# A four-layer diffusion backbone step: the product with the values of an attention unit is issued behind the first scores of the next unit

## The chip, the cores and the metric

The kernel runs on one core of one Trainium2 chip. The metric is the device time of one execution in microseconds (us), the median of three runs. Beside the runs there is one profiled execution, whose trace gives the start, the length and the wait of each instruction.

## What is computed

One inference step of a trunk of four layers with the same weights for 128 context tokens and 512 latent tokens (640 together, width 1024, 16 heads of 64); 128 further context tokens are cached as keys and values. Each layer is: modulated norm, a token mixer, a gated residual, a modulated norm, SwiGLU, a gated residual.

Here `op` is the mixer's output for the context tokens, which see context keys alone, and `os_` that of the latent tokens, which see a selection of latent keys and all cached context keys in one softmax. The mixers of layers 0 to 3 are neighbourhood attention, a sliding window, latent attention with low-rank keys, and grouped-query attention.

```python
for li in range(DEPTH):
    mp = adaln(c_ctx[None, :], w_mod[li], b_mod[li])
    ms = adaln(c, w_mod[li], b_mod[li])
    hp = modulate(rms_norm(xp, norm1_g[li]), mp[0], mp[1])
    hs = modulate(rms_norm(xs, norm1_g[li]), ms[0], ms[1])
    ...
    xp = xp + mp[2] * op
    xs = xs + ms[2] * os_
    xp = xp + mp[5] * swiglu(modulate(rms_norm(xp, norm2_g[li]), mp[3], mp[4]), ffn_w_gate[li], ffn_w_up[li], ffn_w_down[li])
    xs = xs + ms[5] * swiglu(modulate(rms_norm(xs, norm2_g[li]), ms[3], ms[4]), ffn_w_gate[li], ffn_w_up[li], ffn_w_down[li])

def joint_softmax(parts, sink=None):
    s = jnp.concatenate(parts, axis=-1) if len(parts) > 1 else parts[0]
    m = jnp.max(s, axis=-1, keepdims=True)
    ...
    p = jnp.exp(s - m)
    p = p / den
```

## The kernel before

All matrix products are made from pairs of rounded numbers (a high and a low part), so that one product is three matmuls: high by high, low by high, high by low. In the profile they are `whi,hh`, `wlo,hh`, `whi,hl` (or `hh,whi` and so on), and all of them have line 271, the helper `mm`.

The attention of a layer is a loop over 16 **units** (`units`). A unit is a pair of heads and one half of the 512 latent queries: unit u is group u//4, pair u//2 % 2, half u % 2 (`half_pair`). It has four **blocks** (`blocks`, one method for each kind of mixer), each of one head and 128 queries:

1. the scores of the block, queries by keys, into a PSUM tile `S` (`S<-k,q`; in layer 2 `S<-k,qn` and `S<-kpe,qpe`);
2. the softmax on VectorE, ScalarE and GpSimd, which leaves `p`;
3. TensorE turns `p` into `tp` (PSUM, `tp<-consts,p`, line 1009), and ScalarE copies `tp` to `pt` (line 285).

Behind the four blocks comes the **product with the values** (`pv`): `sm<-pt,v` into one PSUM tile `sm`, 16 to 20 matmuls that all read `pt`. For odd units the attention of the context tokens follows in the same tile (`prompt_group`, then `sm<-ptp,v`). Its result, `o`, is copied out by `put_o`. PSUM holds in layers 0 and 1 three `S`, two `tp` and three `sm` tiles, in layers 2 and 3 two `S` of two banks, two `tp` and two `sm`.

Other work is placed between the blocks. `job(gen, n, t0, t1)` spreads the n steps of a generator evenly from time t0 to t1, where the time is the unit plus a quarter per block; `tick` runs before each block. These are the projections of the next group (in layer 2 the `sm<-whi,hh` products of 384 columns), the preparation of keys and queries (`prep_group`, `prep_pair`, transposes `tp<-consts,ktok` and `tp<-consts,qs`), the parts of the output projection (`out_part`, `sm<-hh,whi` of 320 columns, which read the finished `o` of pairs 0 to 4, made ready by `acts`), and parts of the modulation (`mod_parts`, `sm<-rawm,cond`). The keys of a pair are doubled to both halves of the partitions by copies between SBUF tiles on the queue of SyncE (SP), `k<-k`, and the first scores of the next pair read them.

What order the engines get is not the order of the code: a scheduler of the framework emits, on each engine, the instruction with the best priority among those that it holds ready at that time. `high_priority(offset=AHEAD)` pulls an attention block ahead of the filler by 100 places, and `issue_after(x)` forbids an instruction before x. `run_of` binds the matmuls of one accumulation together: the first is placed, and the others follow it.

Of the kernel before, what the change touches and what calls it, by code (L numbers as in the profile page):

```python
# [17 lines left out]
NL = 512  # L18
NP = 128
T = 640  # L20
# [242 lines left out]
class Net:  # L263
# [6 lines left out]
    def mm(self, out, lhsT, rhs, start, stop):  # L270
        return self.nc.tensor.matmul(out, lhsT=lhsT, rhs=rhs, start=start, stop=stop, skip_group_check=True)  # L271
# [593 lines left out]
class Attn:  # L865
# [5 lines left out]
    def __init__(self, net, L):  # L871
        self.net, self.L, self.nc = net, L, net.nc
        self.o, self.V, self.hd = {}, {}, {}
        self.sink = None
        self.jobs, self.events = [], {}
        self.fast = True
# [32 lines left out]
    def units(self):  # L909
        self.fast = False  # L910
        for u in range(16):
            self.half_pair(u // 4, u // 2 % 2, u % 2)
        self.tick(16)
# [180 lines left out]
    def half_pair(self, g, pr, hf):  # L1094
        net = self.net
        u = 4 * g + 2 * pr + hf
        own = self.prompt_group(g, pr) if hf else None
        vals = self.blocks(g, pr, hf, u)
        with net.tc.high_priority(offset=AHEAD):
            o = net.ps()  # L1100
            net.run_of(self.pv(o[:, :256], vals) + (self.pv(o[:, 256:384], own) if hf else []))
            self.put_o(self.o_tile(2 * g + pr), o[:, :256], hf)
            if hf:
                self.put(self.o_tile(2 * g + pr), slice(NL, T), o[:, 256:384])
# [47 lines left out]
class Full(Attn):  # L1152


    def blocks(self, g, pr, hf, u):
# [3 lines left out]
        for b in range(4):  # L1159
            jj, e = b // 2, b % 2  # L1160
            self.tick(u + b / 4)
            with net.tc.high_priority(offset=AHEAD):
                s = net.ps("S")
                for half in range(2):
                    self.scores(4 * g + 2 * pr + e, s[:, half, :320], 2 * hf + jj, half * 320, half * 320 + 320)
                p = self.softmax(s[:, :, :320], T)
# [11 lines left out]
class Mha:  # L1178
# [4 lines left out]
    def body(self):  # L1183
# [11 lines left out]
        self.job(self.acts(self.direct), 5, 12.5 - lead, 13.5 - lead)  # L1195
        self.job(net.out_part(L, 0), 16, max(13.5 - lead, 10) + (0 if L else 0.5), 16)
# [3 lines left out]
        else:  # L1200
            self.at(13.5 - lead, self.load_x)
# [44 lines left out]
class Na(Mha, Attn):  # L1246
# [77 lines left out]
    def blocks(self, g, pr, hf, u):  # L1324
        net = self.net
        pt = self.tile([P, 2, 3, 256], "pt", 2)
        for jj in range(2):
            j = 2 * hf + jj
            w0 = self.win[j][0]
            for e in range(2):  # L1330
# [3 lines left out]
                with net.tc.high_priority(offset=AHEAD):  # L1334
                    s = net.ps("S")[:, :384]
                    self.score(s[:, :256], q, k[:, 0, w0:w0 + 256], k[:, 1, w0:w0 + 256])
                    self.score(s[:, 256:], q, k[:, 0, T:], k[:, 1, T:])
                    p = self.softmax(s, 384, bias[:, (0, 1, 1, 2)[j]])
# [84 lines left out]
class Swa(Gqa, Attn):  # L1423
# [11 lines left out]
    def blocks(self, g, pr, hf, u):  # L1435
        net, k = self.net, self.kg[g]
        pt = self.tile([P, 2, 4, 256], "pt", 2)
        for jj in range(2):
# [10 lines left out]
            for e in range(2):  # L1449
                self.tick(u + (2 * jj + e) / 4)  # L1450
                h = 4 * g + 2 * pr + e
                with net.tc.high_priority(offset=AHEAD):
# [3 lines left out]
                    self.score(s[:, co:co + P], q, k[:, 0, NL:T], k[:, 1, NL:T])  # L1456
                    p = self.softmax(s, w + P, m, (self.sink[0][:, h:h + 1], self.sink[1][:, h:h + 1]))
# [297 lines left out]
```

## Time and profile before

| | us |
|---|---|
| median of 3 runs | 3218.72 |
| lowest and highest | 3214.39, 3223.7 |
| profiled execution | 3216.05 |
| its span (first to last instruction) | 3214.0 |
| attention of layer 0 | 46 to 400 |
| attention of layer 1 | 905 to 1145 |
| attention of layer 2 | 1635 to 1965 |
| attention of layer 3 | 2485 to 2745 |

The mean granted clock of TensorE in the profiled execution is 0.976 of full speed. Between the four stretches of attention lie the output projection, the SwiGLU and the first projections of the next layer. A row of the timeline is a run of like instructions of one engine: its start, the time it took, the instruction and its count, and in brackets how long the engine stood idle before it and which write released it.

### The profile page before, as it was taken

The numbers are of one execution on the slowest core, as the hardware profiler recorded it, in microseconds if no ns is written. First come the engines' busy times: TensorE is split into PE (matmuls) and PEld (weight loads), VectorE is DVE, ScalarE is ACT, GpSimd is POOL, SyncE is SP. The second block draws the span as 40 slices with busy tenths as digits, with TensorE's granted clock in tenths as the row PEclk, the third lists the DMA queues.
The fourth block names the chain that finished last, engine by engine and source line by source line (L and its number), as shares of the span: only waits on it lengthen the run. The fifth ranks groups of instructions, "written<-read, shape, count | busy, mean of one in ns | idle before, by whom it ended". The sixth has DMA issues, their size and how long they took to land.

```text
span 3214.0 us, 57273 instructions
## 1 busy us (share of the span) xinstructions
PE 3029.7 (94%) x21901; PEld 2841.6 (88%) x21901; DVE 2161.6 (67%) x4522; ACT 1528.5 (48%) x3264; POOL 607.1 (19%) x691
## 2 busy tenths in 40 slices
PE   7998989999999989999986899899999999899999
PEld 6997879999988779999985778899998878799999
DVE  5555587666586768585768766867575775875765
ACT  4555454333356755242446664434243576543432
POOL 2553200000044420000025542000001553100000
PEclk9998999999999999999998999999999999899999
DMA  8346563232433342222211224522233111132322
GB/s 265 97 123 208 176 224 102 70 92 94 147 102 128 112 155 76 83 83 76 87 53 37 63 75 143 170 89 80 83 132 118 52 32 32 53 99 70 96 66 86
DMA packets 159027, 331.41 MB, mean 103 GB/s; under 512 B 18592, under 2 KB 40480, under 8 KB 158752
## 3 DMA queue, kind: packets, MB, share of 16 engines
q1 hardware_dynamic: 155584, 323.46, 32.3%
q8 instruction: 173, 2.83, 0.4%
q10 hardware_dynamic: 3168, 4.28, 0.4%
q14 instruction: 102, 0.84, 0.1%
HBM read 303.86 MB, written 4.28 MB: 96 GB/s over the span
## 4 chain that ended last, share of the span: by engine, by line
PE 81%; DVE 8%; DMA 5%; ACT 3%; issue 1%; POOL 1%; SPq 0%; DVEq 0%; ACTq 0%; POOLq 0%
PE big L271 53%; PE sm L271 18%; PE S L271 6%; PE tp L1009 3%; DMA rawm<-in_wmod 3%; DMA k<-k 1%; PE tp L271 1%; DMA raw<-in_wall 1%; DVE st L1030 1%; ACT p L1031 1%; DVE x L603 1%; DVE wlo L319 1%; ACT pt L285 0%; DVE qs L958 0%; DVE hl L999 0%
## 5 line engine op out<-in xcount | busy, mean ns | idle before, releaser
L271 PE MATMUL big<-hh,whi 128*128 128x320 f32 x2720 | 825.4, 313 | 11.7 <-ACT hh L645 5.6
L271 PE MATMUL big<-hl,whi 128*128 128x320 f32 x2720 | 829.0, 311 | 6.3 <-DVE hl L649 3.6
L271 PE MATMUL big<-hh,wlo 128*128 128x320 f32 x2720 | 821.0, 310 | 0.0
L318 ACT CAST whi<-raw 128x512 fp32r<-128x512 f32 (+2 forms) x636 | 383.3, 607 | 709.2 <-PE big L271 554.0
L271 PEld LDWEIGHTS big<-hh,whi 128*128 128x128 f32 x2720 | 508.8, 190 | 25.8 <-ACT hh L645 7.8
L271 PEld LDWEIGHTS big<-hl,whi 128*128 128x128 f32 x2720 | 510.1, 189 | 12.0 <-DVE hl L649 6.2
L271 PEld LDWEIGHTS big<-hh,wlo 128*128 128x128 f32 x2720 | 508.2, 189 | 0.1
L319 POOL TENSOR_TENSOR wlo<-raw,whi 128x512 fp32r<-128x512 f32 (+2 forms) x148 | 196.7, 1342 | 1634.0 <-ACT whi L318 1600.6
L319 DVE TENSOR_TENSOR wlo<-raw,whi 128x512 fp32r<-128x512 f32 (+1 forms) x488 | 325.1, 670 | 142.1 <-ACT whi L318 136.1
L318 ACT CAST whi<-sum 128x512 fp32r<-128x512 f32 x352 | 217.6, 619 | 300.1 <-PE big L271 264.6
L271 PE MATMUL big<-ah,wlo 128*128 128x320 f32 x1408 | 329.1, 309 | 0.0
L271 PE MATMUL big<-ah,whi 128*128 128x320 f32 x1408 | 329.0, 310 | 0.0
L271 PE MATMUL big<-al,whi 128*128 128x320 f32 x1408 | 328.6, 309 | 0.0
L319 DVE TENSOR_TENSOR wlo<-sum,whi 128x512 fp32r<-128x512 f32 x352 | 240.8, 684 | 54.5 <-ACT whi L318 52.9
L1041 POOL TENSOR_SCALAR p<-p,st 128x640 f32<-128x640 f32 (+2 forms) x256 | 197.7, 778 | 285.2 <-DVE st L1040 172.0
L603 DVE SCALAR_TENSOR_TENSOR x<-big,mod,x 128x128 f32<-128x128 f32 (+2 forms) x384 | 146.2, 432 | 150.7 <-PE big L271 150.3
L271 PEld LDWEIGHTS big<-ah,whi 128*128 128x128 f32 x1408 | 237.3, 188 | 1.3 <-issue 0.8
L271 PEld LDWEIGHTS big<-al,whi 128*128 128x128 f32 x1408 | 237.3, 188 | 0.3
L271 PEld LDWEIGHTS big<-ah,wlo 128*128 128x128 f32 x1408 | 237.3, 188 | 0.2
L271 PE MATMUL sm<-whi,hh 128*128 128x256 f32 (+1 forms) x770 | 225.1, 297 | 1.7 <-DVE qs L287 1.1
L271 PE MATMUL sm<-wlo,hh 128*128 128x256 f32 (+1 forms) x770 | 223.3, 292 | 0.2 <-POOL wlo L319 0.2
L271 PE MATMUL sm<-whi,hl 128*128 128x256 f32 (+1 forms) x770 | 223.1, 291 | 0.0
(260 smaller groups left out, 5419.3 us busy)
## 6 DMA issues: line engine op xcount, KB each, us to landing
raw<-in_wall SPq DMA_DIRECT2D x676, 256.0 KB, 2.6
rawm<-in_wmod SPq DMA_DIRECT2D x176, 512.0 KB, 5.8
k<-k SPq DMA_DIRECT2D x38, 384.0 KB, 4.2
bias<-in_nabias SPq DMA_DIRECT2D x16, 576.0 KB, 7.2
raw<-in_wmod SPq DMA_DIRECT2D x32, 256.0 KB, 5.7
qpe<-pes SPq DMA_DIRECT2D x56, 80.0 KB, 2.1
raw<-in_wall SPq DMA_DIRECT2D x32, 128.0 KB, 2.1
out_y<-x ACTq DMA_DIRECT2D x8, 320.0 KB, 2.2
```

The source lines that it names most:

```text
L271: return self.nc.tensor.matmul(out, lhsT=lhsT, rhs=rhs, start=start, stop=stop, skip_group_check=True)
L318: self.nc.scalar.copy(hi, raw)
L319: eng.tensor_tensor(lo, raw, hi.bitcast(F32), ALU.subtract)
L603: self.last = self.nc.vector.scalar_tensor_tensor(xs, halves[b][:, p0:p1], self.mcol(L, i, d, c), xs, ALU.mult, ALU.add)
L1009: self.nc.tensor.transpose(out, in_, self.net.ident)
L1030: nc.vector.tensor_reduce(nm, s, axis=AX.XY, op=ALU.max, negate=True)
L1031: nc.scalar.activation(p.rearrange("p (a b) -> p a b", a=2), s, AF.Exp, bias=nm, accum_out=den)
L1041: nc.gpsimd.tensor_scalar(p, p, rd, 1.0, ALU.mult, ALU.mult)
```

## The change

The product with the values is no longer issued at the end of its unit. `half_pair` wraps it, with the copies that empty it, in a function `product` and keeps that in `late`. In the next unit each `blocks` calls `scores_done` behind the scores of each block; the first such call takes `product` from `late` and runs it, with `issue_after` on the last matmul of those scores. The last unit's product runs behind the loop with no such condition. `self.scored` is reset with each unit.

Since `o` of a pair is thus complete half a block to one unit later, two jobs and the reload of `x` have new times: `acts` runs from 13 - lead to 14 - lead (it was 12.5 to 13.5), and `out_part` and `load_x` start at 14 - lead (13.5 before).

```diff
@@ -268,7 +268,8 @@
 
 
     def mm(self, out, lhsT, rhs, start, stop):
-        return self.nc.tensor.matmul(out, lhsT=lhsT, rhs=rhs, start=start, stop=stop, skip_group_check=True)
+        self.last_mm = self.nc.tensor.matmul(out, lhsT=lhsT, rhs=rhs, start=start, stop=stop, skip_group_check=True)
+        return self.last_mm
 
     def run_of(self, mms):
 
@@ -873,6 +874,7 @@
         self.o, self.V, self.hd = {}, {}, {}
         self.sink = None
         self.jobs, self.events = [], {}
+        self.late, self.scored = [], None
         self.fast = True
 
     def run(self):
@@ -910,6 +912,7 @@
         self.fast = False
         for u in range(16):
             self.half_pair(u // 4, u // 2 % 2, u % 2)
+        self.late.pop()()
         self.tick(16)
 
     def tile(self, shape, tag, bufs=1, dt=F32):
@@ -1096,12 +1099,27 @@
         u = 4 * g + 2 * pr + hf
         own = self.prompt_group(g, pr) if hf else None
         vals = self.blocks(g, pr, hf, u)
-        with net.tc.high_priority(offset=AHEAD):
-            o = net.ps()
-            net.run_of(self.pv(o[:, :256], vals) + (self.pv(o[:, 256:384], own) if hf else []))
-            self.put_o(self.o_tile(2 * g + pr), o[:, :256], hf)
-            if hf:
-                self.put(self.o_tile(2 * g + pr), slice(NL, T), o[:, 256:384])
+
+        def product():
+            with net.tc.high_priority(offset=AHEAD):
+                o = net.ps()
+                mms = self.pv(o[:, :256], vals) + (self.pv(o[:, 256:384], own) if hf else [])
+                if self.scored is None:
+                    net.run_of(mms)
+                else:
+                    with net.tc.issue_after(self.scored.ins):
+                        net.run_of(mms)
+                self.put_o(self.o_tile(2 * g + pr), o[:, :256], hf)
+                if hf:
+                    self.put(self.o_tile(2 * g + pr), slice(NL, T), o[:, 256:384])
+        self.scored = None
+        self.late.append(product)
+
+    def scores_done(self):
+
+        if self.late:
+            self.scored = self.net.last_mm
+            self.late.pop()()
 
     def put_o(self, dst, o, hf):
         self.put(dst, slice(hf * 256, (hf + 1) * 256), o)
@@ -1163,6 +1181,7 @@
                 s = net.ps("S")
                 for half in range(2):
                     self.scores(4 * g + 2 * pr + e, s[:, half, :320], 2 * hf + jj, half * 320, half * 320 + 320)
+                self.scores_done()
                 p = self.softmax(s[:, :, :320], T)
                 for kt in range(5):
                     if n % 4 == 0:
@@ -1192,13 +1211,13 @@
             self.job(self.prep_pair(g, 0), self.pp, 4 * g - mid, 4 * g - end)
         for g in range(4):
             self.job(self.prep_pair(g, 1), self.pp, 4 * g, 4 * g + 1)
-        self.job(self.acts(self.direct), 5, 12.5 - lead, 13.5 - lead)
-        self.job(net.out_part(L, 0), 16, max(13.5 - lead, 10) + (0 if L else 0.5), 16)
+        self.job(self.acts(self.direct), 5, 13 - lead, 14 - lead)
+        self.job(net.out_part(L, 0), 16, 14 - lead + (0 if L else 0.5), 16)
         if L:
             if L == 1:
                 self.job(net.mod_parts(2, 0, 4096, self.ap), 9, 0, 16)
         else:
-            self.at(13.5 - lead, self.load_x)
+            self.at(14 - lead, self.load_x)
             self.job(net.mod_parts(0, 2048, 6144, self.ap), 9, 7, 16)
         self.now(self.prep_group(0), self.prep_pair(0, 0))
         self.units()
@@ -1335,6 +1354,7 @@
                     s = net.ps("S")[:, :384]
                     self.score(s[:, :256], q, k[:, 0, w0:w0 + 256], k[:, 1, w0:w0 + 256])
                     self.score(s[:, 256:], q, k[:, 0, T:], k[:, 1, T:])
+                    self.scores_done()
                     p = self.softmax(s, 384, bias[:, (0, 1, 1, 2)[j]])
                     tp = net.ps("tp")[:, :384]
                     for kt in range(3):
@@ -1454,6 +1474,7 @@
                     q = self.hd[h][:, j * P:(j + 1) * P]
                     self.score(s[:, lo:lo + w], q, k[:, 0, t0 * P:t1 * P], k[:, 1, t0 * P:t1 * P])
                     self.score(s[:, co:co + P], q, k[:, 0, NL:T], k[:, 1, NL:T])
+                    self.scores_done()
                     p = self.softmax(s, w + P, m, (self.sink[0][:, h:h + 1], self.sink[1][:, h:h + 1]))
                     tp = net.ps("tp")[:, :w + P]
                     for i, c in enumerate(cols):
```

The same matmuls are issued, in another order. The rows below are the queue of TensorE as it is written into the program; each row is a line, an operation, the tiles and the shape of the output, with a count where like instructions follow each other (the trace shows a matmul of the kinds `S<-k`, `sm<-pt,v` and `sm<-rawm,cond` as two, so 10 here are x20 there). Of the 60 places between two units of a layer, the next unit's first scores stood ahead of the product in 44 before, and stand ahead of it in all 60 now.

Layer 2, from unit 3 to unit 4 (the units 7 to 8 and 11 to 12 are alike). Before, TensorE's queue from the transposes of `ktok` on:

```order
L1009 MATMUL tp<-consts,ktok 128x128 x6
L1009 MATMUL tp<-consts,p 128x128 x12
L271 MATMUL sm<-pt,v 64x256 x10
L271 MATMUL sm<-ptp,v 64x128 x2
L271 MATMUL sm<-whi,hh 128x384
L271 MATMUL sm<-wlo,hh 128x384
L271 MATMUL sm<-whi,hl 128x384
L271 MATMUL sm<-whi,hh 128x384
L271 MATMUL sm<-wlo,hh 128x384
L271 MATMUL sm<-whi,hl 128x384
L271 MATMUL S<-k,qn 128x320 x2
L271 MATMUL S<-kpe,qpe 128x320
```

And in the changed kernel, from the third of the six products on:

```order
L271 MATMUL sm<-whi,hl 128x384
L271 MATMUL sm<-whi,hh 128x384
L271 MATMUL sm<-wlo,hh 128x384
L271 MATMUL sm<-whi,hl 128x384
L1012 MATMUL tp<-consts,p 128x128 x12
L271 MATMUL S<-k,qn 128x320 x2
L271 MATMUL S<-kpe,qpe 128x320
L271 MATMUL S<-k,qn 128x320 x2
L271 MATMUL S<-kpe,qpe 128x320
L271 MATMUL sm<-pt,v 64x256 x10
L271 MATMUL sm<-ptp,v 64x128 x2
L271 MATMUL S<-k,qn 128x320 x2
```

The six products stand ahead of the transposes `tp<-consts,p` now, and the first four rows of scores of unit 4 (its first block) stand between these and the product with the values `sm<-pt,v`, which came ahead of everything before.

Layer 0, from unit 11 to unit 12, TensorE's queue. Before:

```order
L271 MATMUL sm<-hl,whi 128x320
L271 MATMUL sm<-hh,wlo 128x320
L271 MATMUL sm<-pt,v 64x256 x2
L271 MATMUL sm<-pt,vs 64x128 x4
L271 MATMUL sm<-pt,v 64x128 x4
L271 MATMUL sm<-ptp,v 64x128 x2
L271 MATMUL S<-k,q 128x256 x2
L271 MATMUL S<-k,q 128x128 x2
```

In the changed kernel:

```order
L271 MATMUL sm<-hl,whi 128x320
L271 MATMUL sm<-hh,wlo 128x320
L271 MATMUL S<-k,q 128x256 x2
L271 MATMUL S<-k,q 128x128 x2
L271 MATMUL sm<-pt,v 64x256 x2
L271 MATMUL sm<-pt,vs 64x128 x4
L271 MATMUL sm<-pt,v 64x128 x4
L271 MATMUL sm<-ptp,v 64x128 x2
```

Here the rows `sm<-hh,whi` and its like are the output projection. The first scores of unit 12 moved from behind the product of unit 11 to ahead of it, and of the 24 projections that stood ahead of that product, behind the last transposes of unit 11, 12 are left there.

Layer 1, unit 8, TensorE's queue (`pp` belongs to the context tokens). Before, directly behind the transposes of `qs`:

```order
L1009 MATMUL tp<-consts,p 128x128 x11
L271 MATMUL S<-k,q 128x256 x2
L271 MATMUL S<-k,q 128x128 x2
L1009 MATMUL tp<-consts,pp 128x128 x2
L271 MATMUL S<-k,q 128x256 x2
L271 MATMUL S<-k,q 128x128 x2
L271 MATMUL S<-k,q 128x384 x2
L271 MATMUL S<-k,q 128x128 x2
L1009 MATMUL tp<-consts,p 128x128 x4
L271 MATMUL sm<-pt,v 64x256 x6
L271 MATMUL sm<-pt,v 64x128 x2
L271 MATMUL sm<-rawm,cond 32x256 x16
```

In the changed kernel:

```order
L1012 MATMUL tp<-consts,qs 128x128 x5
L271 MATMUL sm<-rawm,cond 32x256 x16
L1012 MATMUL tp<-consts,p 128x128 x11
L1012 MATMUL tp<-consts,pp 128x128 x2
L271 MATMUL S<-k,q 128x256 x2
L271 MATMUL S<-k,q 128x128 x2
L271 MATMUL S<-k,q 128x256 x2
L271 MATMUL sm<-pt,v 64x256 x6
L271 MATMUL sm<-pt,v 64x128 x2
```

The modulation product `sm<-rawm,cond` moved ahead of the transposes of `p`, directly behind those of `qs`, and two rows of scores stand between the transposes and the product of the unit before.

On SP the copies `k<-k` keep their place relative to the work that makes the keys. At the three places of layer 2 a load of weights (`raw<-in_wall`), which was issued behind them, now stands ahead of them.

## Rows read from the trace of the kernel before

**Rows 1.** Page, part 1: busy us, share of span, instructions.

```profile
PE 3029.7 (94%) x21901; PEld 2841.6 (88%) x21901; DVE 2161.6 (67%) x4522; ACT 1528.5 (48%) x3264; POOL 607.1 (19%) x691
```

**Rows 2.** Windows by stage: length, busy us of each engine, granted clock, DMA share, GB/s.

```profile
46.00:400.00 354.00, 330.84 (x2785) 305.75 (x2786) 193.93 (x502) 182.95 (x454) 140.93 (x169) 0.96 0.51 155
...
1635.00:1965.00 330.00, 277.53 (x1813) 236.56 (x1812) 234.22 (x535) 206.32 (x472) 140.70 (x182) 0.93 0.23 63
```

**Rows 3.** TensorE's waits, whole span: us in total, times, longest us.

```profile
PE sm L271 <- ACT pt L285: 18.4, 18, 2.6
```

**Rows 4.** Timeline of TensorE, layer 0, end of unit 12: start us, us, instruction, idle before.

```profile
337.35 1.98 PE L271 MATMUL sm<-pt,v 128*64 128x256 f32 x12 [2.15 <-ACT pt L285]
```

**Rows 5.** Timeline of TensorE, layer 2, end of unit 3.

```profile
1767.64 1.11 PE L1009 MATMUL tp<-consts,p 128*128 128x128 f32 x4 [1.71 <-ACT pt L285]
1769.43 4.48 PE L271 MATMUL sm<-pt,v 128*64 128x256 f32 x20 [0.68 <-ACT pt L285]
...
1774.05 0.44 PE L271 MATMUL sm<-whi,hh 128*128 128x384 f32 x1
...
1775.21 0.45 PE L271 MATMUL S<-k,qn 128*128 128x320 f32 x2
...
1778.14 0.56 PE L271 MATMUL S<-k,qn 128*128 128x320 f32 x2 [1.01 <-ACT p L1031]
```

**Rows 6.** The k copies of that place on SP: issue and landing.

```profile
L1006 SPq DMA_DIRECT2D k<-k x2: 494/496/497, 1767.1 to 1768.1; - x2
...
DMA to landing us min/median/max: 3.8/4.2/4.5
```

**Rows 7.** Timeline of TensorE, layer 2, end of unit 7.

```profile
1830.58 2.38 PE L271 MATMUL sm<-pt,v 128*64 128x256 f32 x20 [0.68 <-ACT pt L285]
...
1835.52 0.56 PE L271 MATMUL S<-k,qn 128*128 128x320 f32 x2 [0.22 <-DMA k<-k]
...
1837.19 0.55 PE L271 MATMUL S<-k,qn 128*128 128x320 f32 x2 [0.53 <-ACT p L1031]
```

**Rows 8.** Timeline of TensorE, layer 0, end of unit 11.

```profile
313.96 0.31 PE L271 MATMUL sm<-hh,wlo 128*128 128x320 f32 x1
...
315.72 0.31 PE L271 MATMUL sm<-hh,wlo 128*128 128x320 f32 x1
```

**Rows 9.** The k copies of that place on SP: issue and landing.

```profile
L1006 SPq DMA_DIRECT2D k<-k x2: 467/468/468, 305.7 to 306.8; - x2
...
DMA to landing us min/median/max: 10.4/10.5/10.6
```

**Rows 10.** Timeline of TensorE, layer 0, unit 13.

```profile
347.06 0.68 PE L271 MATMUL S<-k,q 128*128 128x256 f32 x4 [1.51 <-DMA k<-k]
```

**Rows 11.** Timeline of TensorE, layer 0, unit 1.

```profile
136.92 0.68 PE L271 MATMUL S<-k,q 128*128 128x256 f32 x4 [1.07 <-DMA k<-k]
```

**Rows 12.** Timeline of TensorE, layer 1, unit 8.

```profile
1058.17 0.95 PE L1009 MATMUL tp<-consts,p 128*128 128x128 f32 x7 [2.59 <-DVE trs L287]
...
1067.93 1.94 PE L271 MATMUL sm<-rawm,cond 128*32 128x256 f32 x32
```

**Rows 13.** Timeline of TensorE, layer 1, end of unit 15.

```profile
1142.97 0.98 PE L1009 MATMUL tp<-consts,p 128*128 128x128 f32 x7 [0.62 <-ACT pt L285]
...
1145.42 3.06 PE L271 MATMUL sm<-pt,v 128*64 128x256 f32 x16 [0.57 <-ACT pt L285]
```

**Rows 14.** TensorE's waits in layer 2's attention, 1635 to 1965 us.

```profile
PE tp L1009 <- ACT pt L285: 9.7, 9, 1.7
...
PE sm L271 <- ACT pt L285: 6.3, 7, 1.7
```

**Rows 15.** Windows of three stretches at half rate.

```profile
275.30:292.30 17.00, 13.12 (x82) 9.68 (x86) 4.43 (x18) 6.94 (x23) 3.00 (x6) 0.50 0.89 247
...
1145.70:1149.00 3.30, 3.30 (x21) 2.06 (x18) 0.00 (x0) 0.06 (x1) 0.00 (x0) 0.50 0.93 320
1766.90:1773.70 6.80, 5.39 (x24) 3.10 (x26) 1.16 (x2) 1.74 (x4) 0.00 (x0) 0.50 0.49 117
```


## The prediction

> **What bounds the kernel now.** Read the page first: TensorE is busy for 94% of the span [rows 1], so a change of order can win idle time of TensorE and little else. Then the windows by stage say how much of that there is where the change works: in layer 0's attention TensorE is busy for 330.84 of 354 us, in layer 2's for 277.53 of 330 [rows 2]. That is 23 and 52 us of idle time, of many kinds. The waits say which kind the change aims at: the product with the values stood idle for the copy `pt` for 18.4 us in 18 places [rows 3]. That is 0.57% of 3216, the most that hiding this wait can give before anything else is counted, and the last product of each layer has no next unit to stand behind. So the view that decides is the timeline around each of the 18, with the order of the instructions beside it: does other work now stand between the last transposes and the product, and is that work itself ready?
>
> **The change part by part.** No instruction of TensorE is added or removed, so nothing is priced but waits that go, come or move. I count a gain as positive.
>
> *Places where nothing moves: 0.* In 44 of 60 places the next scores were already ahead of the product. The long waits of layer 0 are of this kind: the one at 337.35 us waited 2.15 us [rows 4] with unit 13's scores already behind TensorE, and it keeps its neighbours. Of the 18.4 us some 4 lie at the places below and some 2 at the last products of the layers; the other 12 I leave where they are: what is short there is ready work, not permission to take it.
>
> *Layer 2, the products of units 3, 7 and 11: the term with the most in it.* Before, the transposes waited 1.71 us for `pt`, the product 0.68, and the next unit's scores another 1.01 [rows 5]; at unit 7 the like waits are 0.68, 0.22 and 0.53 [rows 7]. In the changed order the six products of 384 columns, 1.16 us between 1774.05 and 1775.21 [rows 5], go ahead of the transposes, and the first block of scores goes between transposes and product. Gone are 3 x 0.68 = 2.0 us of waits before products, two times 1.05 us of waits that the six products now cover (0.1 less than their 1.16, since they ended behind another kind of work; unit 11 has other filler there), and the 1.01 + 0.22 + 0.53 = 1.8 us of the scores behind, in all 5.9. But the scores of unit 4 read the keys that SP copies at 1767.1 us, and the first of the two copies lands 3.8 us after its issue at the soonest [rows 6], at 1770.9. TensorE, which ends its transposes at 1767.64 + 1.11 = 1768.75 [rows 5], stands at the scores until then: a new wait of 2.15 us. Before, product and six products lay in this time. With the like at all three places the loss is 3 x 2.15 = 6.5, and the term is 5.9 - 6.5 = **-0.6**. The price of this wait has two ends: nothing, if the copies go out earlier because the six products end earlier, and 4.5 us each, a whole landing [rows 6], if the weight load that stands ahead of them on SP now holds them up: that is 3 x 2.3 = 7 us more. I take the middle value, since the products that free the weights' buffers end earlier as well.
>
> The trace bears on what can be done in such a wait: at 1835.52 us TensorE waits 0.22 us for a copy of keys with the rest of its queue behind it [rows 7], though filler stood there. The Trainium skill says why this is general, in "PSUM — Partial Sum Buffer", section "Engine vs sequencer instructions": matmuls start and complete in program order. It speaks against the change, since a ready product cannot pass scores that are not ready; were it otherwise, the 6.5 us would be 0 and the term +5.9.
>
> *Layer 0: +0.4.* Between units 11 and 12 TensorE now reaches the scores after 12 projections, not 24: the twelfth starts at 313.96 and the last at 315.72 [rows 8], so at 314.1. The keys were issued at 305.7 and took 10.4 to 10.6 us [rows 9], so they land at 316.2 (316.1 to 316.3): a new wait of 2.1 us, and before there was none. Against this, ahead of unit 14's scores there are 12 projections more than before (36 for 24), 12 x 0.147 = 1.76 us from the same pitch (1.76 us for 12), which covers the wait of 1.51 [rows 10]; and on SP the keys of units 2 and 3 now go ahead of a load of the bias, which I take to win the 1.07 us that the scores waited at 136.92 [rows 11], 0 if it does not. Sum -2.1 + 1.5 + 1.0.
>
> *Layer 1: +3.4.* In unit 8 the modulation products, 1.94 us [rows 12], move into a wait of 2.59 us for the copy `trs` [rows 12]: +1.9. They have to come from somewhere, see the small places below. At the end of unit 15 three waits, the first 0.62 and the last 0.57 us [rows 13], sum 1.5 with the 0.35 between them, have projections put between them in the new order: +1.5.
>
> *Small places, each at the mean wait for `pt` in layer 2's attention, 9.7 / 9 = 1.1 us [rows 14]: -2.0.* This is a common price for unlike places, an estimate from that row. Gains: the context transposes of units 4 and 8 of layer 2 get a block of scores ahead of them (2.2), unit 13's product too (0.7 at 6.3 / 7 = 0.9 less the cover of 0.2). Losses: in layer 2, unit 6 has three blocks of scores in a row, and the end of unit 15 has nothing between its two sets of transposes; in layer 1, unit 0 puts two blocks of scores whose `q` VectorE writes late ahead of the product, and unit 10 lacks the filler that unit 8 took (4.4 together); the end of layer 3 half of one (0.5). 2.9 - 4.9 = -2.0; each place could be between 0 and the longest wait of that row, 1.7.
>
> *The clock: 0, with wide ends.* After a long wait TensorE runs at half of its clock for a while. At 1145.70 us, behind the waits at layer 1's end, 3.3 us at a granted clock of 0.50, the lower of the two levels, 1.2 GHz [rows 15]; behind the wait at 1767.64 the product of unit 3 takes 4.48 us [rows 5] where unit 7's, at full rate, takes 2.38 [rows 7]. A stretch of 3.3 busy us costs half of it, 1.65 us. In layer 0 such a stretch holds 13.12 busy us, 6.6 us lost, of 17.0 [rows 15]. The change may rid us of the one at 1145.70 (+1.65), which had its waits filled, and of that at 1766.90 (5.39 busy, +2.7) [rows 15], and it may put new ones behind the four new waits for keys (4 x 1.65 = 6.6). As the one in layer 0 keeps its causes, I take 0 and hold ±6.6 for the range.
>
> *Sum.* -0.6 + 0.4 + 3.4 - 2.0 + 0 = +1.2 us gained against the profiled execution's 3216.05: 3214.9. The median of the runs shown is 3218.7, 2.7 us above that execution, with a spread from 3214.4 to 3223.7; so a measured time lies some 1 to 2 us above, and I say **3216 us**.
>
> **The rivals.** *(A) The waits go and the clock comes with them.* If the order frees all of the products except the four last ones, 18.4 less some 2.4 = 16 us [rows 3] go, and with them the half-rate stretches that follow such waits, 6.6 + 1.65 + 2.7 = 11 us [rows 15]: 3216 - 27 = 3189 at the most, and some 3200 if half of it holds. For it speaks that each of these stretches does stand behind a wait of this kind; against it that in most places of the 12 us the order does not change. The Trainium skill describes the same chain, waits that send the array to its slow clock, in "TensorE: Matmul & The Clock Gate", section "HAM oscillation — how this bites in real kernels"; by it a removed wait is worth more than its length, as rows 15 bear out with 0.50.
>
> *(B) The product is held behind scores that wait for their keys.* The four places above (layer 2 three times, layer 0 once), each later than I priced it: if the weight load on SP delays the copies by 2.3 us at three places (7 us) and each of the three products behind runs at half rate (4.48 - 2.38 = 2.1, 6.3 us) [rows 5, 7], with 2 us at layer 0's place, it is 15 us: 3231. For it speaks that TensorE had the product to do in just this time; against it that copies of 3.8 us lie in a queue which was idle. It decides, that is reaches 0.3%, when the keys come about 2.5 us later at each of the four than I priced.
>
> *(C) The change does little,* since 44 of 60 places already had that order and the 16 others trade one wait for another. That is my forecast.
>
> **How the numbers follow.** 0.3% is 9.7 us, about what a measurement of this kernel can tell from no change. (C) gets 0.50, and its own range is 3216 ± 9; (A) gets 0.28, some 3189 to 3206; (B) 0.22, some 3226 to 3236. The range that leaves out no more than 2 in 10 takes half of (A)'s and most of (B)'s: 3201 to 3233. By the same cases: faster 0.28, same 0.50, slower 0.22.
>
> **What would show it.** In the changed profile: at the ends of layer 2's units 3, 7 and 11 a wait of some 2 us of `S` for `k<-k`, and none of `sm` for `pt`; at layer 0's unit 12 a wait of 2 us for `k<-k`; at layer 0's other products the same waits for `pt` as before, that of 2.15 us among them; no wait at layer 1's end. The prediction is wrong if the total of `sm` waiting for `pt` falls below 5 us with no waits for `k` in its place (A), or if the copies of keys land more than 4.5 us behind TensorE's arrival (B), or if stretches at 0.50 come or go by more than 7 us in sum.

## The result: slower by 0.6%, and the profile after

The changed kernel took 3236.38 us (3234.47 to 3245.21) where before took 3217.99 in the same comparison: a ratio of 1.0063, interval 1.0049 to 1.0077. Timed once more among the experiments it gave 3232.14 us and a ratio of 1.0046 (1.0029 to 1.0063). So the loss is 14 to 18 us. The profiled execution is the slowest of the first four, 3245.21 us with a span of 3243.4 us; a sum over its trace comes out about 9 us too high for the median, and where it matters the second profile of the same kernel stands beside it.

The page and the waits of TensorE over the whole span, in the changed kernel (us in total, times, longest us):

```profile
PE 3040.6 (94%) x21901; PEld 2852.0 (88%) x21901; DVE 2158.5 (67%) x4522; ACT 1525.8 (47%) x3264; POOL 616.2 (19%) x691
```

```profile
PE sm L271 <- DMA rawm<-in_wmod: 37.3, 15, 5.2
PE S L271 <- DMA k<-k: 24.6, 11, 4.2
...
PE sm L271 <- ACT pt L286: 15.2, 16, 2.6
PE tp L1012 <- ACT pt L286: 13.5, 12, 2.5
```

The wait that the change is about, of products for `pt`, shrank by 3.2 us, from the 18.4 of [rows 3]. The wait of scores for the copies of keys stands at 24.6 us; in the trace of before it was

```profile
PE S L271 <- DMA k<-k: 8.3, 6, 2.5
```

so it grew by 16.3 us. In the second profile of the changed kernel it is 22.1. In the same waits the modulation's loads, `rawm`, count 37.3 us for 27.4 before (33.4 in the second profile).

The end of unit 3 in layer 2, on TensorE's timeline, which answers to [rows 5]:

```profile
1786.76 0.42 PE L271 MATMUL sm<-whi,hh 128*128 128x384 f32 x1
...
1791.45 0.66 PE L1012 MATMUL tp<-consts,p 128*128 128x128 f32 x4 [2.54 <-ACT pt L286]
1794.47 0.90 PE L271 MATMUL S<-k,qn 128*128 128x320 f32 x2 [2.36 <-DMA k<-k]
...
1796.37 3.83 PE L271 MATMUL sm<-pt,v 128*64 128x256 f32 x20
```

and of unit 7, which answers to [rows 7]:

```profile
1852.78 0.66 PE L1012 MATMUL tp<-consts,p 128*128 128x128 f32 x4 [2.03 <-ACT pt L286]
1856.48 0.90 PE L271 MATMUL S<-k,qn 128*128 128x320 f32 x2 [3.04 <-DMA k<-k]
...
1858.38 3.55 PE L271 MATMUL sm<-pt,v 128*64 128x256 f32 x20
```

The reader is to see three things. The product has no bracket any more: its own wait is gone. The scores ahead of it wait 2.36 and 3.04 us for the keys, and the like at unit 11 waits 2.61. And the rows behind the wait are long: the first scores take 0.90 us for 0.45 in [rows 5], and unit 7's product 3.55 us for 2.38. The stage windows show the last point (length, busy us of each engine, granted clock, DMA share, GB/s), for the three such stretches of layer 2:

```profile
1792.00:1799.00 7.00, 4.64 (x21) 3.07 (x22) 6.04 (x19) 2.05 (x7) 1.74 (x3) 0.54 0.56 140
1854.00:1861.00 7.00, 4.52 (x20) 3.16 (x22) 5.83 (x18) 1.52 (x7) 1.74 (x3) 0.52 0.53 141
1919.00:1925.50 6.50, 4.87 (x20) 3.29 (x22) 0.99 (x2) 0.88 (x2) 0.76 (x1) 0.50 0.36 88
```

TensorE ran there near the lower of its levels (0.50 is 1.2 GHz). Unit 3 had such a stretch before [rows 15], and so had unit 11, whose product took 4.07 us before:

```profile
1892.88 4.07 PE L271 MATMUL sm<-pt,v 128*64 128x256 f32 x20 [0.68 <-ACT pt L285]
```

In the changed kernel it takes 3.90 us. Of the three, unit 7's stretch alone is new.

In layer 0's attention, the waits of TensorE (46 to 407 us) hold another new row, and the timeline of TensorE shows its place:

```profile
PE S L271 <- DMA k<-k: 14.1, 5, 4.2
PE sm L271 <- ACT pt L286: 7.3, 6, 2.6
PE big L271 <- DVE hl L1002: 3.5, 1, 3.5
```

```profile
385.65 0.42 PE L271 MATMUL big<-hh,whi 128*128 128x320 f32 x1
389.53 0.50 PE L271 MATMUL big<-hh,whi 128*128 128x320 f32 x1 [3.47 <-DVE hl L1002]
389.83 0.73 PE L271 MATMUL big<-hl,whi 128*128 128x320 f32 x2
```

The second part of layer 0's output projection starts, waits 3.47 us after one matmul for VectorE's split of the last product, and goes on at half rate (0.73 us for two matmuls; the granted clock is 0.52 from 389.5 to 393.0 us). Before, the wait for that split was 0.44 us.

To see which stretch lost the time, the same matmuls were matched between the traces. The lengths against before in us, from the starts of the products of units 0 and 15 in each layer:

| stretch | changed kernel | changed kernel, second profile |
|---|---|---|
| layer 0, unit 0 to 15 | +6.4 | +0.9 |
| layer 0, unit 15, to layer 1, unit 0 | +9.1 | +7.7 |
| layer 1, unit 0 to 15 | +5.2 | -0.2 |
| to layer 2, unit 0 | +1.2 | +1.0 |
| layer 2, unit 0 to 15 | +4.0 | +4.7 |
| to layer 3, unit 0 | +2.3 | +1.1 |
| layer 3, unit 0 to 15 | -0.9 | -0.9 |
| to the last matmul | +1.0 | +1.7 |

Layer 2 and the stretch after layer 0 lose in both, layers 0 and 1 only in the one; layer 3, where nothing was priced but 0.5 us, gains a little. One profile does not settle such a stretch: the two columns are one kernel, and differ by 5.5 us in layer 0 and by 5.4 us in layer 1. Kernels below that leave layers 0 and 1 alone still show +1.8 and +2.6 between layer 0 and layer 1. The ends of the stretches moved too, since a product now stands behind more work than before; taken from the first to the last matmul of the output projection and the SwiGLU (the `big` tiles), the stretch behind layer 0 is 5.4 and 6.7 us longer.

### The profile page after: what moved, and what is told of

Its sections match the earlier page's. It is cut to its first block, busy times and chain, and to the rows that moved or that the text cites. A ratio compares the mean times of both kernels' runs of the same rounds, so it can differ in the third digit from the quotient of the medians.

```text
span 3243.4 us, 57273 instructions
## 1 busy us (share of the span) xinstructions
PE 3040.6 (94%) x21901; PEld 2852.0 (88%) x21901; DVE 2158.5 (67%) x4522; ACT 1525.8 (47%) x3264; POOL 616.2 (19%) x691
## 5 line engine op out<-in xcount | busy, mean ns | idle before, releaser
L271 PE MATMUL big<-hh,whi 128*128 128x320 f32 x2720 | 825.1, 313 | 14.5 <-ACT hh L646 4.4
L271 PEld LDWEIGHTS big<-hl,whi 128*128 128x128 f32 x2720 | 510.3, 189 | 10.6 <-DVE hl L650 6.2
L320 POOL TENSOR_TENSOR wlo<-raw,whi 128x512 fp32r<-128x512 f32 (+2 forms) x148 | 206.3, 1409 | 1607.4 <-ACT whi L319 1566.6
```

Source lines behind the costliest of these rows:

```text
L271: self.last_mm = self.nc.tensor.matmul(out, lhsT=lhsT, rhs=rhs, start=start, stop=stop, skip_group_check=True)
L320: eng.tensor_tensor(lo, raw, hi.bitcast(F32), ALU.subtract)
```

## The experiments

Two theories were set against each other. **K**: the loss is the force. A product that is ready has to stand behind scores whose keys have not landed. **T**: the loss comes from the later times of the output projection, which leave units with less filler. All kernels were timed beside before on the same chip; a ratio is to before, with its interval.

**The times alone.** In `half_pair` the product is run at the end of its unit, and only the times of the jobs are changed.

```diff
-        self.late.append(product)
+        product()
```

> The product stays at the end of its unit; only the two jobs and the reload of x start half a unit later, as in the change. Theory K (the loss is the forced order: products held behind scores whose keys have not landed, in layers 0 and 2): the time of before, 3218 within 5 us. Theory T (the later times of the output projection cost it, since units 9 to 12 lack filler): most of the 18 us, 3230 or more.

Measured: 3226.12 us, ratio 1.0023 (1.0011 to 1.0035). Neither theory had it: the times alone cost some 7.5 us, about half of the loss. In its trace layer 0's attention is 5.7 us longer, and the scores there wait 13.3 us for keys (6.9 before), though no product was deferred.

**The change without the force.**

```diff
-                    with net.tc.issue_after(self.scored.ins):
-                        net.run_of(mms)
+                    net.run_of(mms)
```

> As the change, but without the condition that the product comes behind the scores: the product is still handed to the scheduler after them, and stands ahead of them at the ends of layer 2's units 3, 7 and 11, behind the six products. Theory K: the waits of S for k of 2.4 to 3.0 us at these places shrink by the 2.4 us of the product, and most of the 18 us come back, 3218 to 3224. Theory T, or a loss by the filler's new order: 3230 or more.

Measured: 3223.50 us, 1.0021 (1.0009 to 1.0032), some 9 us under the change as timed second. Product and scores change places at the ends of units 3, 7 and 11 of layer 2, of unit 11 of layer 0 and of unit 0 of layer 1. The filler of layers 1 and 2 moved as well, so this pair does not differ by the force alone. Layer 2's attention (unit 0 to 15) is 3.8 us shorter than before, where the change is 4.0 and 4.7 us longer. Its waits there, 1648 to 1970 us:

```profile
PE sm L271 <- ACT pt L286: 7.5, 7, 1.9
...
PE S L271 <- DMA k<-k: 2.7, 2, 1.4
```

The keys cost 2.7 us there. In the change they cost 9.5, over 1660 to 1990 us:

```profile
PE S L271 <- DMA k<-k: 9.5, 5, 3.0
```

The products wait again, 7.5 us for 6.3 in [rows 14]. So the forced order costs some 8 us in layer 2, as K has it; 5 us more than before remain, as T has it. The half-rate stretch of unit 7 did not go with the wait for keys; without the force its product reads:

```profile
1841.43 4.07 PE L271 MATMUL sm<-pt,v 128*64 128x256 f32 x20 [0.68 <-ACT pt L286]
```

**Only the products of even units deferred**, behind scores whose keys are there.

```diff
-        self.late.append(product)
+        if hf == 0:
+            self.late.append(product)
+        else:
+            product()
```

> Only the products of even units are deferred, so that no product stands behind the first scores of a new pair of heads with new keys; the later times of the jobs stay. Theory K: 3215 to 3223. Theory T: 3230 or more.

Measured: 3216.84 us, 0.9999 (0.9987 to 1.0011). K's number, though the later times stay. What the even products gain must then about pay for the times; that is argued from the 7.5 us of the first experiment, not shown by this run.

**Layer 2 alone** (`if self.L == 2`, and the times of before in the other layers).

> The change in layer 2 alone, whose jobs have no new times. Theory K: three waits of S for k of 2.4 to 3.0 us and a half-rate product behind each, about 8 us more than before, 3224 to 3229. Theory T: the time of before, 3218 within 4.

Measured: 3221.23 us, 1.0014 (1.0000 to 1.0027): slower by 4.5 us by the ratio and not by 8. The median lies inside T's span too, so the time does not decide. The trace does: the waits for keys in layer 2 add up to 10.6 us (1.5 before), and its attention is 5.1 us longer. That nothing is lost here, as T has it, does not hold.

**Layer 0 alone** (`if self.L == 0`, the later times there alone), and **layer 1 alone** in the same way.

> The change in layer 0 alone, with its later times. Theory K+T (two costs that add: products held behind late keys, and in layer 0 the later times): the times' 7 us and some 2 to 5 us of waits for keys, 3227 to 3231. Rival (the cost of layer 0 is the later times alone): 3226. Rival (layer 1 carries a third of the loss): 3222 or less.

Measured: 3222.14 us, 1.0012 (1.0002 to 1.0023). Less than any sum of parts had it; the last rival's number is the nearest.

> The change in layer 1 alone, with its later times. Theory K+T: no keys are copied between pairs there in the same way, so little is lost, 3216 to 3221. Rival (the order of the filler around layer 1's groups costs the 5 us by which its attention grew in the changed kernel's trace): 3223 or more.

Measured: 3221.89 us, 1.0009 (0.9997 to 1.0021). Between the two expectations; inconclusive by itself. The three layers add up to 1.0035, so no single layer holds the loss.

**The times of before, with the deferral and the force in all layers.** `s` is 0.5 in layers 0 and 1 and 0 in layer 3.

```diff
+        s = 0 if L == 3 else 0.5
-        self.job(self.acts(self.direct), 5, 13 - lead, 14 - lead)
-        self.job(net.out_part(L, 0), 16, 14 - lead + (0 if L else 0.5), 16)
+        self.job(self.acts(self.direct), 5, 13 - s - lead, 14 - s - lead)
+        self.job(net.out_part(L, 0), 16, max(14 - s - lead, 10) + (0 if L else 0.5), 16)
...
-            self.at(14 - lead, self.load_x)
+            self.at(14 - s - lead, self.load_x)
```

> The change in all layers, with the times of before in layers 0 and 1 (layer 3 keeps the later ones, since its output projection would otherwise read a pair that is not complete). Theory K+T: 7 us less than the change, 3229. Rival (the later times cost nothing once the products are deferred): 3236.

Measured: 3218.93 us, 1.0003 (0.9989 to 1.0017). More came back than expected, 13 us of the second timing: the deferral with the old times costs nothing that can be told from before, though layer 2 still loses 3.0 us by its trace.

**Only even products, with the times of before.**

> Only the products of even units are deferred, behind scores that read keys that are there already, and all times are those of before. Theory K+T: the run with the later times stood at 3217, 1.6 us under before; without them 7 us less, 3208 to 3213, faster than both kernels. Rival (with the even products deferred the later times cost nothing): 3217.

Measured: 3212.75 us, 0.9990 (0.9978 to 1.0002). In the expected span, 4 us under the same kernel with the later times, and not clear of no change.

**The change again**, for its time.

> The change once more, to have its time by as many runs as the others. Both theories: 3234 to 3238; if it is below 3230, the sum of the parts (2.8 to 7.7 us each) needs no term for their meeting.

Measured: 3232.14 us, 1.0046. Under the expectation by 2 us, and above the sum of the parts (1.0035), though that sum lies in its interval.

**Earlier keys in layer 2**, with the change as it is: the products, the norms and the preparation of the next group's keys run up to half a unit earlier, and `k` has four buffers where it had two (in both places that make it), since two heads hold the other two until their last scores. The two edits were not timed apart.

```diff
-                    self.job(self.products_k(g + 1), 6, 4 * g + 0.75, 4 * g + 1.75)
-                    self.job(self.prep_group(g + 1), 16, 4 * g + 1.75, 4 * g + 2.75)
-                    self.job(self.prep_pair(g + 1, 0), 6, 4 * g + 2.75, 4 * g + 3.5)
+                    self.job(self.products_k(g + 1), 6, 4 * g + 0.75, 4 * g + 1.5)
+                    self.job(self.prep_group(g + 1), 16, 4 * g + 1.5, 4 * g + 2.25)
+                    self.job(self.prep_pair(g + 1, 0), 6, 4 * g + 2.25, 4 * g + 3)
...
-            y = self.tile([P, 2, 768], "k", 2, F32R)
+            y = self.tile([P, 2, 768], "k", 4, F32R)
```

> The change, with the keys of layer 2's next group made half a unit earlier and four buffers for them instead of two, so that they lie ready when the forced scores come. Theory K: the three waits of S for k go, and the 7 to 9 us that the force cost in layer 2's attention with them: 3226 to 3229. Rival (the loss in layer 2 comes from the filler that the new order uses up): 3233 or more.

Measured: 3217.90 us, 1.0003 (0.9992 to 1.0014): 14 us under the change, more than K asked for. The end of unit 3 on TensorE's timeline:

```profile
1784.37 0.54 PE L271 MATMUL S<-k,qn 128*128 128x320 f32 x2
...
1785.33 0.27 PE L1012 MATMUL tp<-consts,p 128*128 128x128 f32 x1
1785.53 2.38 PE L271 MATMUL sm<-pt,v 128*64 128x256 f32 x20
```

No row has a wait, and the product takes its 2.38 us at full rate. In layer 2's attention the products' wait for `pt` is 2.4 us for 6.3 before, that of transposes 4.5 for 9.7 [rows 14], and no wait for keys is in its list. Layer 2's attention is 11.5 us shorter than before, where the change is 4.0 and 4.7 us longer, so by the trace all of the 14 us lie there.

**The control: the same earlier keys in the kernel before.**

> The control: the kernel before with the earlier keys of layer 2 and nothing of the change. Theory K: its first scores were not held up by keys at the ends of units 3, 7 and 11, so the time stays, 3218 within 4. Rival (the earlier keys help by themselves): 8 us or more below.

Measured: 3217.23 us, 0.9997 (0.9987 to 1.0006). No gain from earlier keys by themselves can be told; they are worth 14 us to a kernel that orders work behind them. Earlier keys without the force were not run, so whether the force itself is of use then is not shown.

**No force, and the times of before.**

> The change without the forced order and with the times of before in layers 0 and 1. If force and later times are two costs that add: 3223.5 less the 7 us of the times, 3213 to 3219. If the later times cost only where the order is forced: 3221 to 3225.

Measured: 3214.03 us, 0.9988 (0.9977 to 0.9998): faster than before by 4 us, and 9.5 us under the same kernel with the later times. This is also the cleaner test of the force: with the times of before TensorE's order in layers 0 and 1 is the same with the force and without, and the two kernels differ by 4.9 us (3218.93 and 3214.03). Layer 2's attention is 3.0 us longer than before with the force and 3.1 us shorter without.

So three pairs of kernels that differ in the times alone give 4, 9.5 and 13 us, the first of them not clear of nothing, besides the 7.5 of the first experiment: the later times do cost, and it was left to find where.

**The times of before in layer 0 alone, and in layer 1 alone.**

> The change with the times of before in layer 0 alone. If the later times cost what they do (8 to 13 us) at the end of layer 0's attention (the wait of 3.5 us at the start of the second part of the output projection, and keys that land late beside loads of the modulation): 3221 to 3226. If it is layer 1: 3230 or more.

Measured: 3230.79 us, 1.0056 (1.0037 to 1.0075).

> The counterpart, the times of before in layer 1 alone. If layer 0 carries the cost: 3229 to 3234. If layer 1 does: 3219 to 3226.

Measured: 3229.51 us, 1.0037 (1.0018 to 1.0057). Both lie with the change; neither layer's times give back what the two together do, and with intervals of 6 us either side these two times can't be weighed finely. The traces say more. In layer 0, and in layer 1, several kernels have one and the same order of TensorE, so their traces can be put side by side: the length of a layer's attention against before in us, from the last `big` matmul ahead of it (in layer 0 from the start) to the first behind it.

| attention of | order of the change, later times | deferred, times of before | order of before |
|---|---|---|---|
| layer 0 | mean +4.7 (+0.9 to +8.1, 5 traces) | mean +0.8 (-2.2 to +3.7, 4 traces) | mean +1.1 (-1.3 to +4.8, 4 traces) |
| layer 1 | mean +4.3 (-0.7 to +7.3, 4 traces) | mean -1.3 (-2.1 to -0.1, 3 traces) | mean -1.7 (-3.7 to 0.0, 3 traces) |

So each layer seems to carry some 4 to 6 us of the later times, though traces of one order differ by up to 8 us, and the two kernels that defer even products alone do not show it (+2.9 with the later times and +3.3 without in layer 0, -7.3 with both in layer 1). In the two runs above the layer's own attention did come back (-2.2 and -2.7 us), but layer 2, whose code is that of the change, lost 8.4 and 8.3 us from its first to its last product instead of 4.0 to 4.7. TensorE's order there is another one, and the product of unit 8 takes 4.54 and 4.53 us for 2.38: an edit in one layer lets the scheduler order a later layer anew. So the runs on one layer alone are not clean parts either.

**The PSUM buffers turned by one.** One matmul of one column more into an `sm` tile of its own, ahead of layer 0's last product.

```diff
+        if self.L == 0:
+            net = self.net
+            net.mm(net.ps()[:, :1], self.hd[15][:, :P].bitcast(F32), self.hd[15][:, :1].bitcast(F32), True, True)
         self.late.pop()()
```

> The change, with one matmul of one column more into a PSUM tile of its own ahead of layer 0's last product, so that this product's result lies in another of the three buffers and the second wide accumulator of the output projection takes over a buffer that is free. If that shared buffer is what makes TensorE wait 3.5 us there: the wait goes, and the half-rate stretch behind it, 5 us less than the change, 3226 to 3229. If the wait has another cause: it stays, 3231 to 3236.

Measured: 3233.98 us, 1.0066 (1.0041 to 1.0092). The wait is gone, as TensorE's timeline shows:

```profile
388.55 0.56 PE L271 MATMUL big<-hh,whi 128*128 128x320 f32 x2
388.95 0.46 PE L271 MATMUL big<-hl,whi 128*128 128x320 f32 x2
389.24 0.46 PE L271 MATMUL big<-hh,wlo 128*128 128x320 f32 x2
```

but the time is not lower: the reason for the wait was right, and the 5 us that it should have been worth did not show. With four runs of each kernel a gain of that size is not shut out; but the stretch from layer 0's last product to layer 1's first is 8.9 us longer than before in this trace too, as against 9.1 and 7.7 with the wait. In that profile the scores wait 28.1 us for keys (the change 24.6), so it is a poor trace to weigh one place by.

**Both costs away: earlier keys, and the times of before in layers 0 and 1.**

> The change with both costs taken away: the earlier keys of layer 2 and the times of before in layers 0 and 1. If force behind late keys and later times are two costs that add: the 3218 of the earlier keys less 8 to 13 us, 3205 to 3210, faster than both kernels. If they overlap: 3213 to 3218.

Measured: 3203.43 us, 0.9958 (0.9945 to 0.9970), a little under the expected span, faster than both kernels, and clear of no change. Layer 2's waits, 1650 to 1955 us, show what a deferral looks like where it works:

```profile
PE tp L1013 <- ACT pe L1687: 9.8, 1, 9.8
PE tp L1013 <- ACT pt L286: 5.3, 7, 2.1
PE tp L1013 <- POOL pp L1088: 4.7, 2, 2.9
```

The first row is no matter of the change: it is 9.8 us in the trace of before too. The transposes' wait for `pt` is 5.3 us for 9.7 [rows 14]; waits of products for `pt` and of scores for keys are too small for its first rows. Over the whole span they are 11.0 us (18.4 before) and 14.0 us (8.3 before).

Four kernels now form a square, and the two costs add:

| median in us | keys as they were | earlier keys |
|---|---|---|
| later times | 3232.1 (the change again) | 3217.9 |
| times of before in layers 0 and 1 | 3218.9 | 3203.4 |

Late keys cost 14.2 and 15.5 us, the later times 13.2 and 14.5.

## Why the prediction was wrong, by its steps

*The case.* The forecast was (C), no change at 3216 with a range to 3233; the time was 3236.4, or 3232.1 in the second timing. (C) failed; rival (B), which named 3231 and part of the mechanism, was nearest and had a chance of 0.22. Its number came near in part by luck: it was built on keys some 2.5 us later at each of four places than priced, and they were 0.2, 0.9 and 0.5 us later in layer 2 and hardly later in layer 0; much of the loss came from the later times, which (B) does not name.

*"Places where nothing moves: 0."* Right in the main: products still wait 15.2 us for `pt`. But the wait of 2.15 us that was to keep its neighbours [rows 4] stands at 1.28 us, and that of layer 0's first unit fell from 2.49 to 1.06 us.

*The term of layer 2, -0.6.* Its new waits were sized well: 2.36, 3.04 and 2.61 us of waits for keys against the 2.15 given to each (8.0 against 6.5). Its gains were not. The six products were to cover 1.05 us twice. At unit 3 the three waits ahead of and between the transposes, of which the last was 1.71 us [rows 5], added up to 2.9 us before, and now there is one of 2.54. The transposes wait for copies that follow a chain of their own, and putting work ahead of the first transpose moved the wait and took 0.4 us off it, and at unit 7 0.15 us (2.03 for 0.46 and 1.72). The scores' waits behind the product, 1.01 us at unit 4 and 0.22 and 0.53 at unit 8, were to go; they are 1.97 and 0.78 now. Of the 5.9 us of gains some 1.6 came, nearly all of it the products' own waits. That step, taking a wait as covered by work put ahead of it in the queue, is the one that failed in this term: layer 2's attention lost 4.0 to 4.7 us instead of 0.6, and 8 us lie between it and the kernel without the force. Waits were also priced by their length alone: taking away 9.2 to 9.5 us of waits for keys in layer 2 gave 14 to 16 us back, of which the three products, at 2.38 us again, are about 4.

*"The clock: 0."* The middle was too low. TensorE's busy time, for the same matmuls, is 3040.6 us in the first profile and 3032.6 in the second for 3029.7 [rows 1], 10.9 and 2.9 us more, where the range held ±6.6; the granted clock over the execution is 0.969 and 0.974 for 0.976. Of the two stretches that were to go, that at layer 1's end went (its product takes 1.73 us for 3.06), and that of unit 3 stayed. Unit 7's is new. That the waits for keys bring these stretches is not shown: units 3 and 11 had theirs before, and unit 7's product takes 4.07 us without the force too, behind waits of 2.03 and 0.68 us for `pt`.

*"Layer 0: +0.4."* The new wait at unit 12 came, 1.14 us in the first profile and 2.15 in the second for 2.1. The two gains did not come: unit 14's scores wait 3.90 and 3.07 us for 1.51 [rows 10], and unit 2's 2.24 and 2.47 for 1.07 [rows 11]. In the first profile the copies of keys landed later (12.7 us after the issue at unit 13, 10.2 before). There the last four loads of the modulation begin 4.7 us ahead of the copies, and 6.3 us in the trace of before. That they slow them is argued from this order, not shown by a run.

*The later times were priced at nothing.* They do not appear in the prediction's list of terms at all, other than through the order of units 11 and 13, and cost 7.5 us alone (1.0023) and 4 to 14.5 us in the pairs. This is the second failed step, and the larger one. What in them costs is only partly known. The traces of one order suggest some 4 to 6 us in the attention of each of layers 0 and 1. The wait of 3.47 us at layer 0's end stands only in kernels that have both the later times and the deferral of odd products in that layer; with the times alone it is 0.45 us. Its cause (a PSUM buffer that holds the last product) is shown by the run that removed it, but no gain from that could be told. Which waits make up the rest stays open.

*Layer 1: +3.4.* The gain of 1.5 at its end seems to have come: no wait stands at unit 15 any more, and units 13 to 15 are 4.1 us shorter, though part of that is work that lies in units 9 to 13 now, which are 5.8 to 7.0 us longer. The 1.9 at unit 8 did not show as a shorter stretch: the wait of 2.59 us for `trs` is gone, but three others (0.98, 1.28 and 1.07 us) stand there, 3.3 us for 4.0 before. Here too the cover moved a wait more than it took it away. The layer alone with its times gave 1.0009, not clear of nothing.

The rule of the Trainium skill that the prediction weighed, "PSUM — Partial Sum Buffer", section "Engine vs sequencer instructions" (matmuls start and complete in program order), is borne out by the pair with and without the force: at the end of unit 7 the product stood 3.04 us behind scores without keys; without the force it waits 0.68 us for `pt` there and runs, at half rate, and over the layer 8 us came back. The rule of the Trainium skill in "TensorE: Matmul & The Clock Gate", section "HAM oscillation — how this bites in real kernels", was drawn on for the faster rival only, that a removed wait is worth more than its length. The kernel with the earlier keys goes along with that and does not prove it: 9.2 to 9.5 us of waits for keys went, 14 us came, and the three products take 2.38 us again, but other waits went too. In the change itself the stretches near half rate stood at three of these places instead of two. With both costs away the kernel took 3203 us, near the 3200 of rival (A).

## What to carry to other kernels

Work that is ready may be put behind work that is not only where the second is made early enough: here the deferral cost 14 to 18 us with keys that landed 2 to 3 us late and with later times, and gave some 14 us with keys half a unit earlier and the times untouched in two layers (ratios to before 1.0046 and 0.9958, the earlier keys alone 0.9997). So before an order is forced, follow back the inputs of what is put ahead, to the buffer that lets them be written; and price each change of a start time in the diff as a change of its own, since the time edit here, which layers 0 and 1 could do without, cost as much as the late keys. An expected cover of a wait is to be doubted where the thing waited for depends on the engine that is given other work: here 0.4 and 0.15 us came of 1.05 expected twice. And an edit in one layer can reorder the next ones, so compare the order of the instructions before a part of a change is weighed by itself.

## What was not expected of the hardware

Copies of keys between SBUF tiles, 384 KB each, landed 3.7 to 5.5 us after their issue in layer 2 in the trace of before and up to 14.3 us after it in layer 0 (16.1 in the changed kernel), where loads of weights and modulation run beside them; from kernel to kernel the wait for one and the same copy, that of unit 2's keys in layer 0, was 1.07 us [rows 11], 0.92, 2.57 and 2.70 where the order of TensorE up to there is that of before. That is as much as most terms of the sum. And a single wait of 3.5 us with a stretch at half rate behind it could be taken out of the kernel without a change in its time that four runs could tell.
